# Masked prefix sums and a product: the blind pair in the third place of the ring, two rests a round, the last block summed by columns

## Chip, cores, metric

One core of a Trainium2 chip. The metric is the device time in microseconds of one execution, launch to end; four runs of the kernel before lie within 0.3% (84.62 to 84.87). The profile's span is from the first to the last instruction.

## The reference

```python
B, S, D = 8, 8192, 512          # x: [B, S, D] float32, lengths: [B] int64, w: [D, D]
mask = (pos < lengths[:, None, None])
cs = np.cumsum(x * mask, axis=1)
mid_features = cs[b_idx, lengths // 2, :]
return mid_features @ w          # [B, D]
```

Only one row of each running sum is used, so for each of the eight sequences the first `n = min(length // 2 + 1, length)` rows are summed, and the eight sums are multiplied with `w`. With the drawn lengths `n` is 570, 2690, 256, 2057, 905, 3772, 3859 and 571.

## The kernel before

Rows come in blocks of 512 (1 MB). TensorE sums a block by multiplying it with a matrix of zeros and ones (`cur`) into `s_ps`, four matmuls side by side. What is left of a sequence below 512 rows is a "rest", loaded into `rem` by ScalarE's queue. Two blocks are loaded blind, before the lengths are known, into a buffer of their own:

```python
first = sb("first", [P, BLIND, G, D])
xt = sb("xt", [P, NS, 2, G, D])          # ring of NS = 3 places, a pair of blocks in each
last = sb("last", [P, G, D])
rem = sb("rem", [P, NS, G, D])           # three rests a round
# ...
for b in range(BLIND):
    nc.sync.dma_start(out=first[:, b], in_=xf[b * S:b * S + BLK].rearrange("(p g) d -> p g d", g=G)).then_inc(s_first[b], 16)
```

SyncE loads a pair when its place is free (`s_free`). TensorE sums it, VectorE then writes the place's next weights and frees it:

```python
pe.addr_align(256, offset=80, max_nops=0)     # where TensorE's program starts
# ...
for b in range(BLIND):
    pe.wait_ge(s_first[b], 16)
    for j in range(G):
        add(j, cur_first[:, b], first[:, b, j])
with pe.Fori(0, rounds):
    for k in range(NS):
        pairs(pe, left, add_pair, k, k + 1)       # keep_busy, wait, 4 or 8 matmuls, done
        with pe.If_cmp(some, k + 1, "IS_GE"):     # a rest behind each pair
            take(pe, s_rem[k], 16 * (len(PARTS) + 1))
            # ... four matmuls
```

The last block of the last sequence is loaded at the very end in four pieces (rows 0 and 1 of each group of four, row 2, row 3 left, row 3 right). Its first piece goes into `s_ps` as all blocks do; a tick then releases VectorE, which copies `s_ps` to `s_sb`. The other pieces, and `s_sb` itself, are summed by columns into `t_ps`, which VectorE transposes for the product:

```python
with pe.If_cmp(has_last, 1, "IS_GE"):
    pe.wait_ge(s_last[0], 16)
    for j in range(4):
        add(j, e_last[:], last[:, j // 2], slice(D // 2 * (j % 2), D // 2 * (j % 2 + 1)))
tell()                                            # VectorE may copy s_ps
with pe.If_cmp(has_last, 1, "IS_GE"):
    pe.wait_ge(s_last[1], 16)
    for h in range(2):
        add_columns(h, e_last[:], last[:, 2])
    pe.wait_ge(s_last[2], 16)
    add_columns(0, e_last[:], last[:, 3])
pe.wait_ge(s_dve, DVE_ALL + 1)
add_columns(0, fold[:], s_sb[:]).then_inc(s_pe, 1)
# ... the second half the same way, then the product
```

Of the kernel before, what the change touches and what calls it, by code (L numbers as in the profile page):

```python
# [13 lines left out]
P = 128  # L14
# [3 lines left out]
def kernel(  # L18
# [47 lines left out]
    RR = -(-B // NS)  # L66
# [13 lines left out]
    def sem(name):  # L80
        return tc.alloc_semaphore(name)

    first = sb("first", [P, BLIND, G, D])
    xt = sb("xt", [P, NS, 2, G, D])
    last = sb("last", [P, G, D])
    rem = sb("rem", [P, NS, G, D])
    wt = sb("wt", [P, KC, D])
    lens1 = sb("lens1", [1, 2 * NS * RR], I32)
# [28 lines left out]
    cur_first = sb("cur_first", [P, BLIND, B])  # L117
# [9 lines left out]
    table = sb("table", [P, max(B * (WT + 1), NS * RR * WT)])  # L127
    cur_rem = sb("cur_rem", [P, NS, WT])
# [14 lines left out]
    s_rdone, s_rfree, s_rem = [[sem(f"{n}{q}") for q in range(NS)] for n in ("rdone", "rfree", "rem")]  # L143
    s_last = [sem(f"last{h}") for h in range(len(ENDS))]
    s_first = [sem(f"first{b}") for b in range(BLIND)]
# [14 lines left out]
    def rounds_of(eng, n, least):  # L160

        assert all((i + PER - 1) * 43 >> 8 == -(-i // PER) for i in range(ITEMS))
        to = eng.alloc_register(f"{eng.engine.name}_rounds")
        eng.reg_alu(to, n, PER - 1, ALU.add)
        eng.reg_alu(to, to, 43, ALU.mult)
        eng.reg_alu(to, to, 8, ALU.logical_shift_right)
        eng.reg_alu(to, to, least, ALU.max)
        return eng.snap(to, min_val=least, max_val=ROUNDS)
# [12 lines left out]
    nc.sync.dma_start(out=lens1[:, :2 * B], in_=lens_words).then_inc(s_len1, 16)  # L181
# [5 lines left out]
    for b in range(BLIND):  # L187
        nc.sync.dma_start(
            out=first[:, b], in_=xf[b * S:b * S + BLK].rearrange("(p g) d -> p g d", g=G)
        ).then_inc(s_first[b], 16)  # L190
# [70 lines left out]
    def _(act):  # L261
# [3 lines left out]
        words = [act.alloc_register(f"act_n{i}") for i in range(2 * NS)]  # L265
        pair, top = act.alloc_register("act_pair"), 2 * NS * (RR - 1)
        some = act.alloc_register("act_some")
        act.reg_mov(base, 0)
        act.reg_mov(pair, 0)
        act.reg_mov(some, B)  # L270
        act.memzero(lens1[:, 2 * B:])  # L271
        for q in range(NS):
            act.memzero(rem[:, q]).then_inc(s_rfree[q], 1)  # L273
        act.wait_ge(s_len1, 16)
        with act.Fori(0, RR):
            act.load(words, lens1[:, ds(act.snap(pair, min_val=0, max_val=top), 2 * NS)])
            def rest(q):

                n = words[2 * q]
                alu(t, n, 1, ALU.logical_shift_right)  # L280
                alu(t, t, 1, ALU.add)
                alu(n, t, n, ALU.min)
                take(act, s_rfree[q], 1)
                for count, start, step, g in PARTS:
                    alu(t, n, count, ALU.bitwise_and)
                    with act.If_cmp(t, 1, "IS_GE"):
                        alu(t, n, ~(2 * count - 1), ALU.bitwise_and)
                        act.dma_start(
                            out=rem[start::step, q, :g],
                            in_=rows(act, at, base, t, count).rearrange("(p g) d -> p g d", g=g),  # L290
                        ).then_inc(s_rem[q], 16)
                    with act.Else():
                        act.sem_inc(s_rem[q], 16)
                alu(at, n, ~63, ALU.bitwise_and)
                alu(at, at, base, ALU.add)
                alu(t, n, 63, ALU.bitwise_and)

                def load_last(count):
                    to = rem[3::4, q, 2:] if count > 32 else rem[3:4 * count:4, q, 2:3]
                    act.dma_start(  # L300
                        out=to,
                        in_=xf[ds(act.snap(at), count)].rearrange("(g p) d -> p g d", g=to.shape[1]),
                    ).then_inc(s_rem[q], 16)

                with act.If_cmp(t, 33, "IS_GE"):
                    load_last(64)
                with act.Else():
                    with act.If_cmp(t, 17, "IS_GE"):
                        load_last(32)
                    with act.Else():  # L310
                        with act.If_cmp(t, 1, "IS_GE"):
                            load_last(16)
                        with act.Else():
                            act.sem_inc(s_rem[q], 16)
                alu(base, base, S, ALU.add)
            for q in range(NS):
                if q < B - NS * (RR - 1):
                    rest(q)
                else:
                    with act.If_cmp(some, q + 1, "IS_GE"):  # L320
                        rest(q)
            less(act, some, NS)
            alu(pair, pair, 2 * NS, ALU.add)
            alu(pair, pair, top, ALU.min)
# [10 lines left out]
    def _(pool):  # L335
# [9 lines left out]
        for k in range(NS):  # L345
            pool.sem_inc(s_free[k], 1)
# [4 lines left out]
    def _(dve):  # L351
# [21 lines left out]
        step(dve.tensor_copy, out=len_f[:], in_=lens1[:, :2 * B:2])  # L373
# [8 lines left out]
        def addresses(a, b):  # L382
# [8 lines left out]
        step(dve.tensor_tensor, out=above[:], in0=shape(lens1[:, :2 * B:2].unsqueeze(2), 1, B, K), in1=steps[:],  # L391
# [15 lines left out]
        step(dve.memset, cur_first[:], 0.0)  # L407
# [13 lines left out]
        step(dve.tensor_copy, out=cur_first[:].rearrange("p k b -> p (k b)")[:, ::B + 1], in_=has[:, :BLIND])  # L421
# [6 lines left out]
        step(dve.tensor_tensor, out=cur[:].rearrange("p k h b -> p b (k h)"), in0=since[:, :B, BLIND:BLIND + PER],  # L428
             in1=since[:, 1:, BLIND:BLIND + PER], op=ALU.subtract)
# [14 lines left out]
        tab = table[:, :B * (WT + 1)].rearrange("p (b q) -> p b q", b=B)  # L444
# [4 lines left out]
        rests = table[:, :NS * RR * WT].rearrange("p (r q w) -> p r q w", q=NS, w=WT)  # L449
# [18 lines left out]
        dve.reg_mov(at, BLIND + PER)  # L468
        dve.reg_mov(of, 1)
        dve.reg_mov(some, B - NS)  # L470
        with dve.Fori(1, rounds_of(dve, left, RR)):
            less(dve, left, PER)

            def weights(k):
                take(dve, s_done[k], 1)
                here = ds(dve.snap(at, min_val=BLIND + PER, max_val=ITEMS - PER) + 2 * k, 2)
                dve.tensor_tensor(  # L477
                    out=cur[:, k], in0=since[:, :B, here].rearrange("p b h -> p h b"),
                    in1=since[:, 1:, here].rearrange("p b h -> p h b"), op=ALU.subtract,
                ).then_inc(s_free[k], 1)  # L480

            for k in range(NS):
                pairs(dve, left, weights, k, k + 1)
                with dve.If_cmp(some, k + 1, "IS_GE"):
                    take(dve, s_rdone[k], 1)
                    dve.tensor_copy(  # L486
                        out=cur_rem[:, k],
                        in_=rests[:, ds(dve.snap(of, min_val=1, max_val=RR - 1), 1), k].rearrange("p o w -> p (o w)"),
                    ).then_inc(s_rfree[k], 1)
            less(dve, some, NS)  # L490
            dve.reg_alu(at, at, PER, ALU.add)
            dve.reg_alu(at, at, ITEMS - PER, ALU.min)
            dve.reg_alu(of, of, 1, ALU.add)
            dve.reg_alu(of, of, RR - 1, ALU.min)
# [15 lines left out]
    def _(pe):  # L510
        def add(j, weights, rows, columns=slice(0, D)):

            return pe.matmul(s_ps[32 * j:32 * j + B, columns], lhsT=weights, rhs=rows[:, columns],  # L513
# [30 lines left out]
        left, some, has_last = [pe.alloc_register(f"pe_{n}") for n in ("left", "some", "has")]  # L544
        pe.wait_ge(s_dve, DVE_FIRST)
        pe.load([has_last, left], addr[:, :2])
        pe.reg_mov(some, B)
        rounds = rounds_of(pe, left, RR)
        for b in range(BLIND):
            pe.wait_ge(s_first[b], 16)  # L550
            for j in range(G):
                add(j, cur_first[:, b], first[:, b, j])
        BUSY = [3, 1, 0]
        pe.wait_ge(s_dve, DVE_MASK)
        with pe.Fori(0, rounds):
# [10 lines left out]
            for k in range(NS):  # L566
                pairs(pe, left, add_pair, k, k + 1)
                with pe.If_cmp(some, k + 1, "IS_GE"):
                    take(pe, s_rem[k], 16 * (len(PARTS) + 1))
                    for j in range(G):  # L570
                        mm = add(j, cur_rem[:, k, j * B:(j + 1) * B], rem[:, k, j])
                    mm.then_inc(s_rdone[k], 1)
            less(pe, left, PER)
            less(pe, some, NS)

        with pe.If_cmp(has_last, 1, "IS_GE"):
            pe.wait_ge(s_last[0], 16)
            for j in range(4):
                add(j, e_last[:], last[:, j // 2], slice(D // 2 * (j % 2), D // 2 * (j % 2 + 1)))
        tell()  # L580
        with pe.If_cmp(has_last, 1, "IS_GE"):
            pe.wait_ge(s_last[1], 16)
            for h in range(2):
                add_columns(h, e_last[:], last[:, 2])
# [52 lines left out]
```

## Time and profile before

| | before |
|---|---|
| time, median of the runs until then | 84.75 us |
| span | 82.4 us |
| moved by DMA | 31.25 MB, all engines full from 2.1 to 76.2 us |
| last ordinary block on TensorE | 74.82 us |
| first transpose | 77.37 us |

The prediction shows the slices and the tail. What it uses besides is when SyncE issues its loads (columns: start, duration, engine, line, operation). The first of these lines is the first load into the third place, the second the first refill of the ring:

```profile
10.48 0.34 SPq L222 DMA_DIRECT2D xt<-in_x_dram  x1
19.70 0.34 SPq L222 DMA_DIRECT2D xt<-in_x_dram  x1
```

### The profile page before, as it was taken

To read this page: it belongs to the slowest core of one execution; us is meant where nothing else is said; L and a number is where in the kernel's file an instruction comes from. 1 tells how busy PE (TensorE), PEld (TensorE's weight loads), DVE (VectorE), ACT (ScalarE), POOL (GpSimd) and SP (SyncE) were. 2 spreads that over 40 slices of the span, in tenths; PEclk is the share of its full clock that TensorE was granted. 3 is DMA by queue.
4 is the path that set the end of the run, shared out by engine and by line. 5 is a ranking of instruction groups with operands and counts; after the bars stand their busy time and mean duration, and the time that the engine had idled before them with its cause. 6 is when DMAs were issued, how large, how long until landed. Compare 5 with 4: busy or idle time off the path is not lost. (4 is left out here: it accounts for less than half of the span.)

```text
span 82.4 us, 1513 instructions
## 1 busy us (share of the span) xinstructions
PE 57.7 (70%) x389; PEld 15.1 (18%) x389; DVE 15.0 (18%) x79; ACT 7.4 (9%) x8; POOL 1.3 (2%) x14
## 2 busy tenths in 40 slices
PE   2800699589089699992198099999957989196920
PEld 2300005021021114120011021422201422011510
DVE  2758887001000100010000000000000000000620
ACT  0999300000000000000000000000000000000020
POOL 5000000000000000000000000000000000000000
PEclk9999999999965999999858957999999999999997
DMA  1999999999999999999999999999999999999000
GB/s 18 360 396 420 461 406 429 462 418 398 450 438 404 392 461 390 406 424 408 448 404 422 434 453 419 433 414 438 438 398 461 430 398 453 390 402 377 17 2 6
DMA packets 3826, 31.25 MB, mean 379 GB/s; under 512 B 562, under 2 KB 834, under 8 KB 1618
## 3 DMA queue, kind: packets, MB, share of 16 engines
q1 hardware_dynamic: 2754, 27.27, 78.8%
q10 hardware_dynamic: 1072, 3.97, 12.4%
HBM read 31.23 MB, written 0.02 MB: 379 GB/s over the span
## 5 line engine op out<-in xcount | busy, mean ns | idle before, releaser
L513 PE MATMUL s_ps<-xt,cur 128*8 128x512 f32 x184 | 26.5, 699 | 14.3 <-PEq L151 14.3
L528 PE MATMUL idle_ps<-idle 128*128 128x512 f32 x32 | 16.2, 628 | 0.0
L513 PEld LDWEIGHTS s_ps<-xt,cur 128*8 128x8 f32 x184 | 4.3, 94 | 33.5 <-issue 33.5
L477 DVE TENSOR_TENSOR cur<-since 128x16 f32 x9 | 1.7, 188 | 44.4 <-DVEq L151 44.4
L513 PE MATMUL s_ps<-rem,cur_rem 128*8 128x512 f32 x64 | 8.6, 610 | 0.0
L528 PEld LDWEIGHTS idle_ps<-idle 128*128 128x128 f32 x32 | 5.6, 196 | 11.7 <-issue 11.7
L513 PE MATMUL s_ps<-first,cur_first 128*8 128x512 f32 x16 | 3.6, 1040 | 5.0 <-DVE since L360 5.0
L329 ACT COPY o_sb<-o_ps 8x128 f32<-8x128 f32 x2 | 0.5, 260 | 69.9 <-PE o_ps L600 69.9
L273 ACT ACTIVATE rem<-rem 128x2048 uint32<-128x2048 uint32 x3 | 5.5, 1892 | 0.0
L513 PEld LDWEIGHTS s_ps<-rem,cur_rem 128*8 128x8 f32 x64 | 2.0, 102 | 7.0 <-issue 7.0
L539 PE MATMUL s_ps<-zero 1*128 1x512 f32 x2 | 2.1, 1137 | 1.6 <-DVE zero L360 1.6
L360 DVE COPY s_sb<-s_ps 128x256 f32<-128x256 f32 x2 | 0.8, 424 | 11.6 <-PE idle_ps L532 11.5
L486 DVE COPY cur_rem<-table 128x32 f32 x5 | 0.9, 182 | 3.2 <-DVEq L151 3.2
L513 PEld LDWEIGHTS s_ps<-first,cur_first 128*8 128x8 f32 x16 | 0.2, 89 | 6.7 <-issue 5.1
L271 ACT ACT_TABLE_LOAD x1 | 1.3, 1283 | 1.9 <-issue 1.9
L600 PE MATMUL o_ps<-wt,t_sb 128*8 128x128 f32 x32 | 1.1, 273 | 0.1
L360 DVE TENSOR_TENSOR part_a<-since,step_a 1x42 f32<-1x42 f32 (+1 forms) x2 | 1.1, 565 | 0.1
L521 PE MATMUL t_ps<-last,e_last 128*8 128x64 f32 x32 | 1.0, 220 | 0.1
L360 DVE TENSOR_TENSOR since<-item,begin 1x42 f32<-1x42 int32 (+1 forms) x2 | 0.8, 422 | 0.1
L600 PEld LDWEIGHTS o_ps<-wt,t_sb 128*8 128x8 f32 x32 | 0.8, 89 | 0.3 <-issue 0.3
L542 PEld LDWEIGHTS n_ps<-len_f,ones 1*128 1x128 f32 x2 | 0.7, 332 | 1.0 <-DVE above L360 0.5
L539 PEld LDWEIGHTS s_ps<-zero 1*128 1x128 f32 x2 | 0.5, 306 | 1.6 <-DVE zero L360 1.6
(70 smaller groups left out, 14.3 us busy)
## 6 DMA issues: line engine op xcount, KB each, us to landing
xt<-in_x_dram SPq DMA_DIRECT2D x10, 2048.0 KB, 12.4
xt<-in_x_dram SPq DMA_DIRECT2D x3, 1024.0 KB, 9.5
first<-in_x_dram SPq DMA_DIRECT2D x2, 1024.0 KB, 7.6
rem<-in_x_dram ACTq DMA_DIRECT2D x3, 512.0 KB, 8.6
wt<-in_w_dram ACTq DMA_DIRECT2D x2, 512.0 KB, 5.5
rem<-in_x_dram ACTq DMA_DIRECT2D x3, 256.0 KB, 7.6
last<-in_x_dram SPq DMA_DIRECT2D x1, 512.0 KB, 7.6
rem<-in_x_dram ACTq DMA_DIRECT2D x3, 128.0 KB, 8.0
```

What stands on the lines that cost most here:

```text
L271: act.memzero(lens1[:, 2 * B:])
L273: act.memzero(rem[:, q]).then_inc(s_rfree[q], 1)
L329: copy = act.copy(out=o_sb[1][:, j * P:(j + 1) * P], in_=o_ps[64 + 32 * j:64 + 32 * j + B, :P])
L360: do(*args, **kw).then_inc(s_dve, 1)
L477: dve.tensor_tensor(out=cur[:, k], in0=since[:, :B, here].rearrange("p b h -> p h b"), in1=since[:, 1:, here].rearrange("p b h -> p h b"), ...
L486: dve.tensor_copy(out=cur_rem[:, k], in_=rests[:, ds(dve.snap(of, min_val=1, max_val=RR - 1), 1), k].rearrange("p o w -> p (o w)"),).then_ ...
L513: return pe.matmul(s_ps[32 * j:32 * j + B, columns], lhsT=weights, rhs=rows[:, columns], start=False, stop=False, skip_group_check=True, t ...
L521: mm = pe.matmul(t_ps[h][32 * j:32 * j + B, :P // 2], lhsT=weights, rhs=row[:, at:at + P // 2], start=False, stop=False, skip_group_check= ...
L528: pe.matmul(idle_ps[:], lhsT=idle[:], rhs=idle[:, :1].to_broadcast((P, D)), start=True, stop=True)
L539: pe.matmul(s_ps[:], lhsT=zero[:], rhs=zero[:, :1].to_broadcast((1, D)), start=True, stop=False, skip_group_check=True)
L542: pe.matmul(n_ps[:, :B], lhsT=ones[:], rhs=len_f[:], start=True, stop=True).then_inc(s_pe, 1)
L600: mm = pe.matmul(o_ps[32 * j:32 * j + B, :P], lhsT=t_sb[:, kc, :B], rhs=wt[:, kc, j * P:(j + 1) * P], start=(kc == 0), stop=(kc == KC - 1) ...
```

## The change

Intent: save the separate buffer and the separate code of the blind blocks by treating them as a pair that already stands in the third place, with a loop round of its own; take two rests a round instead of three; and take the last block's first piece off the way of the tick, by summing all its rows by columns.

```diff
-    RR = -(-B // NS)
+    NR = 2
+    RR = -(-B // NR)
-    first = sb("first", [P, BLIND, G, D])
-    rem = sb("rem", [P, NS, G, D])
+    rem = sb("rem", [P, NR, G, D])
     for b in range(BLIND):
         nc.sync.dma_start(
-            out=first[:, b], in_=...
-        ).then_inc(s_first[b], 16)
+            out=xt[:, NS - 1, b], in_=...
+        ).then_inc(s_full[NS - 1], 16)
 # ... GpSimd frees places 0 and 1 only; VectorE, behind its set-up:
+        pairs(dve, left, weights, NS - 1)
 # ... TensorE:
-        with pe.Fori(0, rounds):
-            for k in range(NS):
-                pairs(pe, left, add_pair, k, k + 1)
-                with pe.If_cmp(some, k + 1, "IS_GE"):
+        with pe.Fori(0, rounds_of(pe, left, RR + 1)):
+            with pe.If_cmp(begun, 1, "IS_GE"):
+                pe.wait_ge(s_dve, DVE_MASK)
+                for k in range(NR):
+                    pairs(pe, left, add_pair, k, k + 1)
+                    with pe.If_cmp(some, k + 1, "IS_GE"):
 # ...
+            pairs(pe, left, add_pair, NS - 1)
+            pe.reg_mov(begun, 1)
-        with pe.If_cmp(has_last, 1, "IS_GE"):
-            pe.wait_ge(s_last[0], 16)
-            for j in range(4):
-                add(j, e_last[:], last[:, j // 2], slice(...))
         tell()
         with pe.If_cmp(has_last, 1, "IS_GE"):
-            pe.wait_ge(s_last[1], 16)
-            for h in range(2):
-                add_columns(h, e_last[:], last[:, 2])
+            for i, some in enumerate(([0, 1], [2])):
+                pe.wait_ge(s_last[i], 16)
+                for g in some:
+                    for h in range(2):
+                        add_columns(h, e_last[:], last[:, g])
```

More of the change, by code (lines that the diff above doesn't have):

```diff
@@ L81, in sem @@
         return tc.alloc_semaphore(name)
-    first = sb("first", [P, BLIND, G, D])
     xt = sb("xt", [P, NS, 2, G, D])
     last = sb("last", [P, G, D])
-    rem = sb("rem", [P, NS, G, D])
+    rem = sb("rem", [P, NR, G, D])
     wt = sb("wt", [P, KC, D])
-    lens1 = sb("lens1", [1, 2 * NS * RR], I32)
+    lens1 = sb("lens1", [1, 2 * B], I32)
     len_f = sb("len_f", [1, B])
@@ L116 @@
     row_last = sb("row_last", [1, 1], I32)
-    cur_first = sb("cur_first", [P, BLIND, B])
     cur = sb("cur", [P, NS, 2, B])
@@ L126 @@
     thr = sb("thr", [P, G], I32)
-    table = sb("table", [P, max(B * (WT + 1), NS * RR * WT)])
-    cur_rem = sb("cur_rem", [P, NS, WT])
+    table = sb("table", [P, B * (WT + 1)])
+    cur_rem = sb("cur_rem", [P, NR, WT])
     fold_i = sb("fold_i", [P, B], I32)
@@ L142 @@
     s_done, s_free, s_full = [[sem(f"{n}{k}") for k in range(NS)] for n in ("done", "free", "full")]
-    s_rdone, s_rfree, s_rem = [[sem(f"{n}{q}") for q in range(NS)] for n in ("rdone", "rfree", "rem")]
+    s_rdone, s_rfree, s_rem = [[sem(f"{n}{q}") for q in range(NR)] for n in ("rdone", "rfree", "rem")]
     s_last = [sem(f"last{h}") for h in range(len(ENDS))]
-    s_first = [sem(f"first{b}") for b in range(BLIND)]
     s_w, s_len1, s_out = sem("w"), sem("len1"), sem("out")
@@ L167, in rounds_of @@
         eng.reg_alu(to, to, least, ALU.max)
-        return eng.snap(to, min_val=least, max_val=ROUNDS)
+        return eng.snap(to, min_val=least, max_val=ROUNDS + 1)
     def less(eng, n, by):
@@ L178 @@
     PE_ALL, PE_SUM, PE_OUT = 2, 3, 5
-    nc.sync.dma_start(out=lens1[:, :2 * B], in_=lens_words).then_inc(s_len1, 16)
+    nc.sync.dma_start(out=lens1[:], in_=lens_words).then_inc(s_len1, 16)
     for h in range(2):
@@ L188 @@
         nc.sync.dma_start(
-            out=first[:, b], in_=xf[b * S:b * S + BLK].rearrange("(p g) d -> p g d", g=G)
-        ).then_inc(s_first[b], 16)
+            out=xt[:, NS - 1, b], in_=xf[b * S:b * S + BLK].rearrange("(p g) d -> p g d", g=G)
+        ).then_inc(s_full[NS - 1], 16)
     block = nc.Block(no_gpsimd_drain=True)
@@ L264, in _ @@
         base, at, t = [act.alloc_register(f"act_{n}") for n in ("base", "at", "t")]
-        words = [act.alloc_register(f"act_n{i}") for i in range(2 * NS)]
-        pair, top = act.alloc_register("act_pair"), 2 * NS * (RR - 1)
-        some = act.alloc_register("act_some")
+        words = [act.alloc_register(f"act_n{i}") for i in range(2 * NR)]
+        pair, top = act.alloc_register("act_pair"), 2 * NR * (RR - 1)
         act.reg_mov(base, 0)
         act.reg_mov(pair, 0)
-        act.reg_mov(some, B)
-        act.memzero(lens1[:, 2 * B:])
-        for q in range(NS):
+        for q in range(NR):
             act.memzero(rem[:, q]).then_inc(s_rfree[q], 1)
@@ L275, in _ @@
         with act.Fori(0, RR):
-            act.load(words, lens1[:, ds(act.snap(pair, min_val=0, max_val=top), 2 * NS)])
+            act.load(words, lens1[:, ds(act.snap(pair, min_val=0, max_val=top), 2 * NR)])
             def rest(q):
@@ L315, in rest @@
                 alu(base, base, S, ALU.add)
-            for q in range(NS):
-                if q < B - NS * (RR - 1):
-                    rest(q)
-                else:
-                    with act.If_cmp(some, q + 1, "IS_GE"):
-                        rest(q)
-            less(act, some, NS)
-            alu(pair, pair, 2 * NS, ALU.add)
+            for q in range(NR):
+                rest(q)
+            alu(pair, pair, 2 * NR, ALU.add)
             alu(pair, pair, top, ALU.min)
@@ L344, in _ @@
         pool.iota(fold_i[:], pattern=[[-1, B]], base=128, channel_multiplier=1).then_inc(s_pool, 1)
-        for k in range(NS):
+        for k in range(NS - 1):
             pool.sem_inc(s_free[k], 1)
@@ L372, in _ @@
         dve.wait_ge(s_len1, 16)
-        step(dve.tensor_copy, out=len_f[:], in_=lens1[:, :2 * B:2])
+        step(dve.tensor_copy, out=len_f[:], in_=lens1[:, ::2])
         assert done == DVE_N, done
@@ L390, in _ @@
         dve.wait_ge(s_pool, 1)
-        step(dve.tensor_tensor, out=above[:], in0=shape(lens1[:, :2 * B:2].unsqueeze(2), 1, B, K), in1=steps[:],
+        step(dve.tensor_tensor, out=above[:], in0=shape(lens1[:, ::2].unsqueeze(2), 1, B, K), in1=steps[:],
              op=ALU.is_ge)
@@ L406, in _ @@
         step(dve.memset, since[:, B:], 0.0)
-        step(dve.memset, cur_first[:], 0.0)
+        step(dve.memset, cur[:], 0.0)
         step(dve.memset, bits[:], 256)
@@ L419, in _ @@
              op0=ALU.is_ge, op1=ALU.mult)
-        step(dve.tensor_copy, out=cur_first[:].rearrange("p k b -> p (k b)")[:, ::B + 1], in_=has[:, :BLIND])
+        step(dve.tensor_copy, out=cur[:, NS - 1].rearrange("p h b -> p (h b)")[:, ::B + 1], in_=has[:, :BLIND])
         step(dve.tensor_copy, out=addr[:, :1], in_=has[:1, B - 1:])
@@ L427, in _ @@
         sinces(begin, 0, ITEMS)
-        step(dve.tensor_tensor, out=cur[:].rearrange("p k h b -> p b (k h)"), in0=since[:, :B, BLIND:BLIND + PER],
-             in1=since[:, 1:, BLIND:BLIND + PER], op=ALU.subtract)
+        step(dve.tensor_tensor, out=cur[:, :NS - 1].rearrange("p k h b -> p b (k h)"),
+             in0=since[:, :B, BLIND:PER], in1=since[:, 1:, BLIND:PER], op=ALU.subtract)
         step(dve.tensor_scalar, out=m4[:], in0=pid[:], scalar1=3, scalar2=None, op0=ALU.bitwise_and)
@@ L443, in _ @@
         step(dve.tensor_tensor, out=thr[:, 2:], in0=thr_i[:], in1=shape(m4[:], P, 2), op=ALU.mult)
-        tab = table[:, :B * (WT + 1)].rearrange("p (b q) -> p b q", b=B)
+        tab = table[:].rearrange("p (b q) -> p b q", b=B)
         step(dve.tensor_tensor, out=cap[:], in0=shape(cnt[:].unsqueeze(2), P, B, G),
@@ L448, in _ @@
              in1=shape(thr[:].unsqueeze(1), P, B, G), op=ALU.is_gt)
-        rests = table[:, :NS * RR * WT].rearrange("p (r q w) -> p r q w", q=NS, w=WT)
+        rests = table[:, :B * WT].rearrange("p (r q w) -> p r q w", q=NR, w=WT)
         step(dve.tensor_copy, out=cur_rem[:], in_=rests[:, 0])
@@ L467, in _ @@
         dve.load([left], addr[:, 1:2])
-        dve.reg_mov(at, BLIND + PER)
+        dve.reg_mov(at, BLIND)
         dve.reg_mov(of, 1)
-        dve.reg_mov(some, B - NS)
-        with dve.Fori(1, rounds_of(dve, left, RR)):
-            less(dve, left, PER)
-            def weights(k):
-                take(dve, s_done[k], 1)
-                here = ds(dve.snap(at, min_val=BLIND + PER, max_val=ITEMS - PER) + 2 * k, 2)
-                dve.tensor_tensor(
-                    out=cur[:, k], in0=since[:, :B, here].rearrange("p b h -> p h b"),
-                    in1=since[:, 1:, here].rearrange("p b h -> p h b"), op=ALU.subtract,
-                ).then_inc(s_free[k], 1)
+        dve.reg_mov(some, B - NR)
@@ new lines, in _, with weights @@
+        rounds = rounds_of(dve, left, RR)
+        def weights(k):
+            take(dve, s_done[k], 1)
+            here = ds(dve.snap(at, min_val=BLIND, max_val=ITEMS - PER) + 2 * k, 2)
+            dve.tensor_tensor(
+                out=cur[:, k], in0=since[:, :B, here].rearrange("p b h -> p h b"),
+                in1=since[:, 1:, here].rearrange("p b h -> p h b"), op=ALU.subtract,
+            ).then_inc(s_free[k], 1)
+        pairs(dve, left, weights, NS - 1)
+        with dve.Fori(1, rounds):
+            less(dve, left, PER)
+            dve.reg_alu(at, at, PER, ALU.add)
+            dve.reg_alu(at, at, ITEMS - PER, ALU.min)
@@ L482, in _ @@
             for k in range(NS):
                 pairs(dve, left, weights, k, k + 1)
-                with dve.If_cmp(some, k + 1, "IS_GE"):
-                    take(dve, s_rdone[k], 1)
-                    dve.tensor_copy(
-                        out=cur_rem[:, k],
-                        in_=rests[:, ds(dve.snap(of, min_val=1, max_val=RR - 1), 1), k].rearrange("p o w -> p (o w)"),
-                    ).then_inc(s_rfree[k], 1)
-            less(dve, some, NS)
-            dve.reg_alu(at, at, PER, ALU.add)
@@ L492, in _ @@
-            dve.reg_alu(at, at, ITEMS - PER, ALU.min)
+                if k < NR:
+                    with dve.If_cmp(some, k + 1, "IS_GE"):
+                        take(dve, s_rdone[k], 1)
+                        dve.tensor_copy(
+                            out=cur_rem[:, k],
+                            in_=rests[:, ds(dve.snap(of, min_val=1, max_val=RR - 1), 1), k].rearrange("p o w -> p (o w)"),
+                        ).then_inc(s_rfree[k], 1)
+            less(dve, some, NR)
             dve.reg_alu(of, of, 1, ALU.add)
@@ L510, in _, with add @@
     def _(pe):
-        def add(j, weights, rows, columns=slice(0, D)):
-            return pe.matmul(s_ps[32 * j:32 * j + B, columns], lhsT=weights, rhs=rows[:, columns],
+        def add(j, weights, rows):
+            return pe.matmul(s_ps[32 * j:32 * j + B], lhsT=weights, rhs=rows,
                              start=False, stop=False, skip_group_check=True,
@@ L543, in _ @@
         pe.wait_ge(s_pool, 2)
-        left, some, has_last = [pe.alloc_register(f"pe_{n}") for n in ("left", "some", "has")]
+        left, some, has_last, begun = [pe.alloc_register(f"pe_{n}") for n in ("left", "some", "has", "begun")]
+        pe.reg_mov(some, B)
+        pe.reg_mov(begun, 0)
         pe.wait_ge(s_dve, DVE_FIRST)
         pe.load([has_last, left], addr[:, :2])
-        pe.reg_mov(some, B)
-        rounds = rounds_of(pe, left, RR)
-        for b in range(BLIND):
-            pe.wait_ge(s_first[b], 16)
-            for j in range(G):
-                add(j, cur_first[:, b], first[:, b, j])
+        pe.reg_alu(left, left, PER, ALU.add)
         BUSY = [3, 1, 0]
-        pe.wait_ge(s_dve, DVE_MASK)
-        with pe.Fori(0, rounds):
+        with pe.Fori(0, rounds_of(pe, left, RR + 1)):
             def add_pair(k):
@@ L564, in add_pair @@
                 mm.then_inc(s_done[k], 1)
-            for k in range(NS):
-                pairs(pe, left, add_pair, k, k + 1)
-                with pe.If_cmp(some, k + 1, "IS_GE"):
-                    take(pe, s_rem[k], 16 * (len(PARTS) + 1))
-                    for j in range(G):
-                        mm = add(j, cur_rem[:, k, j * B:(j + 1) * B], rem[:, k, j])
-                    mm.then_inc(s_rdone[k], 1)
-            less(pe, left, PER)
-            less(pe, some, NS)
-        with pe.If_cmp(has_last, 1, "IS_GE"):
-            pe.wait_ge(s_last[0], 16)
-            for j in range(4):
-                add(j, e_last[:], last[:, j // 2], slice(D // 2 * (j % 2), D // 2 * (j % 2 + 1)))
+            with pe.If_cmp(begun, 1, "IS_GE"):
[3 more added lines that the diff above has]
+                    with pe.If_cmp(some, k + 1, "IS_GE"):
+                        take(pe, s_rem[k], 16 * (len(PARTS) + 1))
+                        for j in range(G):
+                            mm = add(j, cur_rem[:, k, j * B:(j + 1) * B], rem[:, k, j])
+                        mm.then_inc(s_rdone[k], 1)
+                less(pe, some, NR)
+            pairs(pe, left, add_pair, NS - 1)
+            less(pe, left, PER)
+            pe.reg_mov(begun, 1)
         tell()
         with pe.If_cmp(has_last, 1, "IS_GE"):
-            pe.wait_ge(s_last[1], 16)
-            for h in range(2):
-                add_columns(h, e_last[:], last[:, 2])
+            for i, some in enumerate(([0, 1], [2])):
[3 more added lines that the diff above has]
+                        add_columns(h, e_last[:], last[:, g])
             pe.wait_ge(s_last[2], 16)
```

## The prediction

> **What bounds the kernel now.** I read the page first, its slices by time and its DMA queues.
>
> ```profile
> PE   2800699589089699992198099999957989196920
> DMA  1999999999999999999999999999999999999000
> GB/s 18 360 396 420 461 406 429 462 418 398 450 438 404 392 461 390 406 424 408 448 404 422 434 453 419 433 414 438 438 398 461 430 398 453 390 402 377 17 2 6
> q1 hardware_dynamic: 2754, 27.27, 78.8%
> q10 hardware_dynamic: 1072, 3.97, 12.4%
> ```
>
> One slice is 82.4/40 = 2.06 us. The sixteen DMA engines are full from the second slice to the 37th (2.1 to 76.2 us), and the two queues add up to 91.2% of 16 engines' span, 75 us: all of that time. TensorE shows a nine often too, but with gaps throughout, and 16.2 us of its work are matmuls on `idle`[...]. So the kernel is a 31.25 MB transfer at about 420 GB/s, with a head of some 2 us before the stream starts and a tail of some 6 us after it. A change can gain only by (a) fewer bytes, (b) fewer holes in the stream, (c) a shorter tail.
>
> The DMA queue's own waits, that is those of the engine that issues the loads, say why the stream has no holes:
>
> ```profile
> SPq L151 <- SPq L151: 32.0, 9, 6.6
> SPq L239 <- DVE fold L360: 3.6, 1, 3.6
> ```
>
> It stands 32 us waiting for a place in the ring of three pairs, with work for the engines already queued. So a place freed a microsecond later costs nothing until the queue behind it runs empty.
>
> The tail I read from the timeline of its last microseconds (start, duration, engine, what, and in brackets the idle time before it):
>
> ```profile
> 74.82 1.04 PE L513 MATMUL s_ps<-xt,cur 128*8 128x512 f32 x8 [0.74 <-PEq L151]
> 75.69 0.62 PE L513 MATMUL s_ps<-last,e_last 128*8 128x256 f32 x8
> 76.13 0.17 PE L532 MATMUL idle_ps<-tick 128*1 128x1 bf16 x1
> 76.36 0.49 PEld L521 LDWEIGHTS t_ps<-last,e_last 128*8 128x8 f32 x24 [0.37 <-DMA last<-in_x_dram]
> 76.39 0.88 DVE L360 COPY s_sb<-s_ps 128x256 f32<-128x256 f32 x2 [11.53 <-PE idle_ps L532]
> 77.32 0.30 PE L521 MATMUL t_ps<-s_sb,fold 128*8 128x64 f32 x8
> 77.37 0.61 DVE L360 STREAM_TRANSPOSE t_sb<-t_ps 128x64 f32<-128x64 f32 x2
> 77.77 1.06 PE L600 MATMUL o_ps<-wt,t_sb 128*8 128x128 f32 x32
> ```
>
> The last ordinary block reaches TensorE at 74.82, the first half of the last block is added by 76.13, then comes the tick that lets VectorE copy `s_ps`. The two copies end at 77.27; only then can VectorE start the transposes (77.37), and the product follows. In that half microsecond the copies bind, not the transfer: by the windows the DMA share is 1.03 in 75 to 76 us, 0.32 in 76 to 77 and 0 after it.
>
> [...]
>
> **The change part by part.**
>
> *Bytes.* By the diff the same loads are issued: 2 blind blocks, 12 pairs (10 as one load of 2048 KB, one as two, and a single block), 8 rests, the last block in four. Nothing is saved or added: 0 us.
>
> *The third place starts occupied.* Before, the load into it was issued at 10.48 us. Now it waits until both blind blocks have been summed and VectorE has written new weights.
> - TensorE: the blind blocks landed 6.3 and 8.9 us after their issues at 1.3 and 1.7, so the second is there at 10.6. Before, the first one's 8 matmul passes ran from 8.87, while the second still came; now all 16 start at 10.6 and take about 3.6 us[...]. They end near 14.2 instead of 12.5.
> - VectorE: it must first finish its set-up, whose last step ended at 14.62, then load registers and branch. TensorE needed 1.3 us for the like (from 7.53 to its first matmul at 8.86). Then the 0.19 us subtraction: free at about 16.2.
> - Issue: before, from a place freed at 19.12 to the load at 19.70 is 0.58 us. So the load goes out near 17 us, 6.5 us later than before, with data about 1.5 us on (the first issues at 0.9 met a full stream only after 2.06): 18.3 us.
> - What lies queued until then, in decimal MB: weights 1.05, blind 2.10, two pairs 4.19, the two rests 0.43, together 7.77. The stream of before had moved 5.8 MB by 16 us and 7.46 by 20 (windows of 2 us: 16, 344, 389, 426, 479, 427, 433, 393, 446, 377 GB/s), so the queue would run dry at about 20.7 us. That is 2.4 us after the new data start. On paper the cost is **0**. I chose to charge **0.1 us**, as the engines don't run level: the second pair was summed only from 23.03 although the bytes ahead of it had passed some 2 us before, so a few engines may stand still briefly.
> - TensorE then does its three keep-busy rounds (3.15 us) from 14.2, so the first pair starts at about 17.3, not 16.72. The load that follows it goes out near 20.2, not 19.70, with a whole pair still queued: **0**.
>
> *Two rests a round.* Eight rests take four rounds instead of three. The pairs take four rounds anyway (23 blocks in rounds of six), and the last rests are summed in the last of them. A rest lands 6 to 8 us after its issue and has a round of about 15 us for it. ScalarE has two memzeros instead of three (1.89 us each) and issues its first rest earlier: before the queues drain, so **0**.
>
> *The blind round.* TensorE runs its loop five times; the extra branches fall where it waits for the blind data: **0**.
>
> *The tail.* Four 256-column matmuls (8 passes, 75.69 to 76.13, 0.44 us) become sixteen 64-column ones behind the tick. The 24 passes in the fence load in 0.49 us, 20.4 ns each, so 32 passes are 0.65 us.
> - The tick moves from 76.13 to 75.69, the copies from 76.39 to about 75.95, and end at 76.83 instead of 77.27.
> - TensorE: 32 passes to 76.35; the third row group (landed about 76.33), 16 passes, to 76.68; the first half of the fourth, 8 passes, to 76.84; fold of the first half to 77.00; last columns to 77.17; second fold to 77.33.
> - The first transpose needs the first fold's end, 76.84 + 0.30 = 77.14, plus the same 0.1 us: 77.24 instead of 77.37. The product and the rest follow, each earlier by **0.13 us**.
>
> So the gain is not the 0.44 us that VectorE wins, as TensorE's longer column work becomes the wait. Sum: -0.13 + 0.1, about 0; from 84.75 I say **84.7 us**.
>
> **The rivals.**
> - *The stream gets a hole* because two pairs instead of three lie queued at the start. For it: the place is freed 6.5 us later, and VectorE's long set-up stands before it. Against it: 2.4 us of reserve. If data come at 21.5 us rather than 18.3, it costs up to 0.8 us: 85.5. A hole would cost its whole length, since the stream is the bound.
> - *TensorE becomes the bound of the tail*: if small column passes run slower than 20.4 ns, at say 30, the 56 passes ahead of the first fold cost 0.5 us more: 85.2. Against it: these very passes are in the trace before.
> - *The stream gets better or worse by itself*, as the rests mix in another order with the pairs: slices vary from 390 to 462 GB/s. One per cent of 74 us is 0.7 us, either way; 84.0 to 85.4.
> - *A full tail gain of 0.44 us*, if the last pieces land earlier so that TensorE is never behind: 84.3.
>
> **Range and chances.** The runs before span 0.25 us. With the mix worth ±0.7 and a hole possibly 0.8, I take 84.0 to 85.4. Two per cent is 1.7 us: no rival alone brings it. Faster by more than 2% would need fewer bytes or a higher rate: 2%. Slower by more than 2% needs a hole of 1.7 us: 4%. Within 2%: 94%.
>
> **What would show it.** In the changed trace: the load into the third place issued at about 17 us; the GB/s of the slices between 14 and 24 us still near 420 (a slice under 300 shows the hole); the DMA bytes still 31.25 MB, the stream ending near 76.3; the tick directly behind the last block's matmuls, 0.4 us earlier relative to them; the first transpose about 2.4 us after the last ordinary block's first matmul (before 2.55). I am wrong if the stream ends over 0.5 us from 76.3, or if column passes take more than 0.65 us for the first half.

-0.13 us for the tail and +0.1 us charged for a brief stand of some engines come to about 0, and from 84.75 to 84.7 us. The 3.6 us for the blind pair are the 3.64 us that its 16 passes took in the profile before (1040 ns each, where the rests' take 610). That the DMA engines don't run level was an estimate from the sums at 23.03 us; the trace doesn't record which engine moved what.

## The result

The changed kernel took 84.07 us (84.00 to 84.18, 4 runs), the kernel before 84.73 us (84.62 to 84.87, 4 runs). The ratio is 0.992 (95% interval 0.990 to 0.994). A ratio here is the mean time of one kernel's fast runs over that of the other's in the same rounds, so it is not quite the ratio of the medians. Executions over 1.5% slower than the fastest of the same kernel are left out of the means. Measured once more with more runs (below) it was 0.995 (0.992 to 0.998): a gain of 0.4 to 0.7 us, inside the predicted range, at its lower end.

The page of the changed kernel, slices and queues:

```profile
GB/s 20 355 414 420 440 438 427 441 414 398 462 414 434 426 422 370 426 450 426 430 406 418 454 382 452 434 408 422 442 420 420 402 450 454 370 410 379 27 0 8
q1 hardware_dynamic: 2754, 27.27, 79.0%
q10 hardware_dynamic: 1072, 3.97, 12.3%
```

The bytes are the same, and no slice between 14 and 24 us (the seventh to the twelfth) falls under 398: the stream has no hole. The head, from the timelines (TensorE's blind pair and its keep-busy matmuls, VectorE's weights that free the third place, the load into it):

```profile
11.00 3.60 PE L506 MATMUL s_ps<-xt,cur 128*8 128x512 f32 x16 [7.12 <-DVE thr L350]
14.53 2.85 PE L521 MATMUL idle_ps<-idle 128*128 128x512 f32 x6
16.20 0.18 DVE L466 TENSOR_TENSOR cur<-since 128x16 f32 x1 [1.62 <-DVEq L149]
16.95 0.34 SPq L220 DMA_DIRECT2D xt<-in_x_dram  x1
```

The load goes out at 16.95 us, where the prediction said "near 17". The tail:

```profile
74.93 1.05 PE L506 MATMUL s_ps<-xt,cur 128*8 128x512 f32 x8
75.79 0.17 PE L525 MATMUL idle_ps<-tick 128*1 128x1 bf16 x1
75.81 0.45 PEld L514 LDWEIGHTS t_ps<-last,e_last 128*8 128x8 f32 x32 [0.30 <-DMA last<-in_x_dram]
76.08 0.88 DVE L350 COPY s_sb<-s_ps 128x256 f32<-128x256 f32 x2 [10.46 <-PE idle_ps L525]
76.50 0.45 PEld L514 LDWEIGHTS t_ps<-last,e_last 128*8 128x8 f32 x24 [0.23 <-DMA last<-in_x_dram]
77.31 0.60 DVE L350 STREAM_TRANSPOSE t_sb<-t_ps 128x64 f32<-128x64 f32 x2 [0.35 <-PE t_ps L514]
```

The stream delivers the last ordinary block 0.11 us later than in the profile before (74.93, 74.82), the tick follows it at once, and the first transpose starts 2.38 us after that block's first matmul instead of 2.55: 0.17 us gained. So the two profiles differ by 0.1 us of span. The gain of the runs is larger than that of the profiled pair: this is what the experiments had to look into.

### The profile page after: what moved, and what is told of

Read it like the earlier page. It is cut to its first block, busy times and chain, and to the rows that moved or that the text cites. A ratio compares the mean times of both kernels' runs of the same rounds, so it can differ in the third digit from the quotient of the medians.

```text
span 82.3 us, 1574 instructions
## 1 busy us (share of the span) xinstructions
PE 55.7 (68%) x413; PEld 15.6 (19%) x413; DVE 15.3 (19%) x81; ACT 5.5 (7%) x6; POOL 1.3 (2%) x14
## 2 busy tenths in 40 slices
DMA packets 3826, 31.25 MB, mean 380 GB/s; under 512 B 562, under 2 KB 834, under 8 KB 1618
## 3 DMA queue, kind: packets, MB, share of 16 engines
q1 hardware_dynamic: 2754, 27.27, 79.0%
## 5 line engine op out<-in xcount | busy, mean ns | idle before, releaser
L506 PE MATMUL s_ps<-xt,cur 128*8 128x512 f32 x200 | 28.0, 681 | 21.3 <-PEq L149 14.2
L521 PE MATMUL idle_ps<-idle 128*128 128x512 f32 x32 | 16.8, 648 | 0.0
L268 ACT ACTIVATE rem<-rem 128x2048 uint32<-128x2048 uint32 x2 | 3.7, 1901 | 0.0
L514 PE MATMUL t_ps<-last,e_last 128*8 128x64 f32 x64 | 1.6, 220 | 0.0
L514 PEld LDWEIGHTS t_ps<-last,e_last 128*8 128x8 f32 x64 | 0.9, 88 | 0.7 <-DMA last<-in_x_dram 0.5
L350 DVE TENSOR_REDUCE sum_a<-part_a 1x6 f32<-1x42 f32 (+1 forms) x2 | 0.8, 381 | 0.1
```

Source lines behind the costliest of these rows:

```text
L268: act.memzero(rem[:, q]).then_inc(s_rfree[q], 1)
L350: do(*args, **kw).then_inc(s_dve, 1)
L506: return pe.matmul(s_ps[32 * j:32 * j + B], lhsT=weights, rhs=rows, start=False, stop=False, skip_group_check=True, tile_position=(0, 32 * j))
L514: mm = pe.matmul(t_ps[h][32 * j:32 * j + B, :P // 2], lhsT=weights, rhs=row[:, at:at + P // 2], start=False, stop=False, skip_group_check= ...
L521: pe.matmul(idle_ps[:], lhsT=idle[:], rhs=idle[:, :1].to_broadcast((P, D)), start=True, stop=True)
```

## The experiments

Two theories at the start. **A**: the whole gain is the tail. **B**: the tail gives what its trace shows, and the rest comes from the stream, through the occupied third place or through the later rests. The first four runs take the parts one by one; all ran on one chip with five rounds.

### The tail alone

The kernel before, with only the last hunk of the diff above.

> The kernel before with the new tail alone (all rows of the last block by columns behind the tick; blind blocks in their own buffer, three rests a round). Theory A, the whole gain of 0.66 us (84.73 to 84.07) is the tail: 84.1 us, ratio 0.992. Theory B, the tail gives only the 0.13 us worked out in the prediction and the rest comes from an earlier end of the stream: 84.6 us, ratio 0.998. The first transpose should come some 2.4 us after the first matmul of the last ordinary block (before 2.55).

Measured: 85.31 us, ratio 1.008 (1.005 to 1.012): 0.8% longer, clear of the noise. Neither theory had this. The tail itself works as it should; the last ordinary block came late:

```profile
76.41 1.04 PE L513 MATMUL s_ps<-xt,cur 128*8 128x512 f32 x8 [0.73 <-PEq L151]
78.77 0.61 DVE L360 STREAM_TRANSPOSE t_sb<-t_ps 128x64 f32<-128x64 f32 x2 [0.34 <-PE t_ps L521]
```

From one to the other are 2.36 us, as in the changed kernel; but the block is there 1.6 us later than before (76.41, 74.82). All six runs have spans of 83.3 to 83.8 us. The page names one queue that the pages of before and of the changed kernel lack. From the DMA view of 32 to 34 us (packets, MB, share of sixteen engines):

```profile
q8 instruction: 1, 0.02, 3.3%
```

One instruction transfer, beside the stream. 3.3% of 16 engines' 2 us are 1.06 us of one engine. And the windows at the end (length; busy times of PE, PEld, DVE, ACT and POOL; granted clock; DMA share; GB/s) show a share of about one engine still at work, here against the changed kernel, which is the second fence:

```profile
76.75:77.50 0.75, 0.75 (x25) 0.31 (x21) 0.00 (x0) 0.00 (x0) 0.00 (x0) 1.00 0.07 26
```

```profile
76.75:77.50 0.75, 0.75 (x44) 0.46 (x32) 0.40 (x2) 0.00 (x0) 0.00 (x0) 1.00 0.00 0
```

A share of 0.06 to 0.07 is about one engine of sixteen. Which one, the trace doesn't record; that it is the engine of the transfer is inferred. The kernel waits for all sixteen counts of a load (`wait_ge(s_last[0], 16)`), and the trace has sixteen landings for that load, in the changed kernel from 75.19 to 75.77 us. So the last of the sixteen decides when a load is there.

### The old tail in the changed kernel

The changed kernel with the old hunk of the tail put back.

> The changed kernel with the old tail (first half of the last block into s_ps ahead of the tick). Theory A: no gain left, 84.7 us, ratio 1.000. Theory B: most of the gain stays, 84.2 us, ratio 0.994, with the first transpose about 2.55 us after the last ordinary block's first matmul.

Measured: 84.54 us, ratio 1.000 (0.996 to 1.004). The profile has the old tail's length, 77.49 less 74.93 = 2.56 us:

```profile
74.93 1.04 PE L506 MATMUL s_ps<-xt,cur 128*8 128x512 f32 x8
77.49 0.60 DVE L350 STREAM_TRANSPOSE t_sb<-t_ps 128x64 f32<-128x64 f32 x2
```

So theory B falls in the form that I gave it: the other two parts together bring no gain that this resolves. The new tail gains with them and didn't without them; why, the next runs try to find out.

### Two rests a round alone

The kernel before with `NR = 2`, everything else as before.

> The kernel before with two rests a round alone (blind blocks keep their own buffer, old tail). Theory A: 84.7 us, ratio 1.000. Theory B with the rests' later loads as its cause (they mix with the pairs over the whole stream): 84.3 us, ratio 0.994. Theory B with the occupied third place as its cause: 84.7, ratio 1.000.

Measured: 84.55 us, ratio 0.998 (0.994 to 1.003). No effect resolved.

### The blind pair in the third place alone

The changed kernel with `NR = 3`, the third rest behind the third pair, and the old tail.

> The kernel before with the blind pair in the third place alone (three rests a round as before, the third rest behind the third pair, old tail). Theory A: 84.7 us, ratio 1.000. Theory B with the occupied third place as its cause: 84.3 us, ratio 0.994; with the rests as its cause: 84.7 us, ratio 1.000. The third place's first load goes out near 17 us in either case.

Measured: 84.44 us, ratio 0.998 (0.995 to 1.001); the load into the third place went out at 16.99 us. No effect resolved, as the prediction had it.

### What the other parts do for the tail

The new tail needs 12 matmuls more in TensorE's program. The two other parts save exactly as many: 4 for the third rest and 8 for the blind blocks. I counted the matmuls in the built programs: 95 before, 95 in the changed kernel, 107 with the tail alone. Each fp32 matmul is four instructions (the ring's 23 blocks, four matmuls each, are 184 weight loads and 184 passes on the page of before), and behind the alignment directive the three programs have 444, 443 and 489 instructions. With a start at slot 80 they end at slots 524, 523 and 569; the last instructions of before and of the changed kernel run after the product. The next expectations rest on an assumption of mine that no run had shown: that a program which ends early enough brings no instruction transfer into the stream.

Hence **theory F**: placement and length of TensorE's program decide whether an instruction transfer falls into the stream, and such a transfer costs about a microsecond (by the spans of the tail alone, 83.53 less 82.48). Its rival **G**: the longer column work disturbs the stream in some other way. The next runs move programs without altering an instruction.

### The changed kernel again

> The changed kernel once more, unaltered. Its runs so far had spans of 82.1 to 82.4 us where the kernel before had 82.2 to 82.6 in most of its runs, so the spans differ by some 0.15 us, while the times outside the span scatter by 0.6 us. If the -0.66 us of the first four runs was part scatter: 84.3 to 84.4 us, ratio 0.995 to 0.998. If it is real: 84.0, ratio 0.992.

Measured: 84.14 us (84.03 to 84.28, 6 runs), before 84.56 (11 runs), ratio 0.995 (0.992 to 0.998). The spans are 82.2 to 82.5 us (mean 82.32), those of before 82.4 to 82.6 and once 83.5 (mean 82.56). So of 0.44 us, the difference of the means, 0.24 lie in the span (0.17 of them the tail of the profile, 0.07 more within what single runs scatter), and 0.20 outside it, where before took 1.8 to 2.3 us and the changed kernel 1.75 to 2.0. An instruction transfer shows in this profile too, but only in the window behind 79 us, when the stream has ended; the profile of before has one there as well, at 83.6 us, behind its last instruction. There the stream is not longer: the span of this profile is 82.3 us, that of before 82.4. From the DMA view of before, 83.5 to 84.6 us:

```profile
q8 instruction: 1, 0.02, 5.3%
```

That is 0.93 us of one engine, with no stream beside it.

### The tail alone, placed 48 slots earlier

```diff
-        pe.addr_align(256, offset=80, max_nops=0)
+        pe.addr_align(256, offset=32, max_nops=0)
```

> The tail-only kernel that was 0.8% slower, its TensorE program merely placed 48 instruction slots earlier (offset 32 instead of 80). Theory F: that kernel lost 1.2 us[...]. Then here the instruction transfer is gone from the DMA part of the page, the span is 82.2 to 82.3 us (82.4 less the 0.13 us of the tail), ratio 0.995 to 0.998. Rival G: the longer column work itself, with three rests and separate blind buffers, slows the stream: again 83.5 us of span, ratio 1.008.

Measured: 85.27 us, ratio 1.008 (1.004 to 1.012), spans 83.0 to 83.7. A miss: the transfer did not go away. It came earlier (DMA view of 2 to 3 us):

```profile
q8 instruction: 1, 0.02, 5.7%
```

So an earlier end of the program (slot 521, below the 524 of before) doesn't keep a transfer out of the stream; that part of theory F falls. That the stream is late when a transfer falls into it stands (span 83.33, before 82.56).

### The changed kernel, placed 48 slots later

> The changed kernel with its TensorE program placed 48 slots later (offset 128 instead of 80)[...]. Theory F: one instruction transfer shows in the DMA part of the page, the span is 83.3 to 83.7 us, 1.2 us longer than the changed kernel's, ratio to the kernel before about 1.009. Rival G: no change, span 82.2, ratio 0.995.

Measured: 85.58 us, ratio 1.013 (1.008 to 1.017), spans 83.4 to 83.8. The instructions are those of the changed kernel, so a loss of this size needs no longer column work, and theory G isn't needed. For the tail alone G isn't excluded: no run of it was free of a transfer. In the DMA view of 12 to 14 us, and in the window at the end:

```profile
q8 instruction: 1, 0.02, 3.1%
```

```profile
76.75:77.50 0.75, 0.75 (x12) 0.22 (x8) 0.00 (x0) 0.00 (x0) 0.00 (x0) 1.00 0.06 23
```

### The third place freed late

This tests the step of the prediction that mattered most, the reserve of the queue. Nine memsets on VectorE, each waiting for the one before, stand between its set-up and the blind pair's weights.

```diff
         dve.wait_ge(s_dve, done)
+        for i in range(9):
+            if i:
+                dve.wait_ge(s_late, i)
+            dve.memset(s_sb[:], 0.0).then_inc(s_late, 1)
+        dve.wait_ge(s_late, 9)
```

> The changed kernel with nine extra memsets on VectorE between its set-up and the blind pair's weights (some 5 to 6 us), so that the third place is freed near 22 us instead of 16.4 and its load goes out near 22.5. By the prediction the queues are empty at about 20.7 us and new data come 1.4 us after the issue, near 24: a hole of some 3 us in the stream, seen as slices well under 400 GB/s between 18 and 24 us, and 87 us (ratio 1.03). If a freed place has no such deadline (rival: the engines are never short of work, as the other places refill them), the time stays at 84.3 and the slices near 420.

Measured: 88.32 us, ratio 1.044 (1.040 to 1.047), spans 86.2 to 86.5. The load's issue, and the windows around it:

```profile
22.93 0.34 SPq L221 DMA_DIRECT2D xt<-in_x_dram  x1
```

```profile
18.00:20.00 2.00, 2.00 (x21) 0.56 (x24) 1.46 (x3) 0.00 (x0) 0.00 (x0) 1.00 1.04 442
20.00:22.00 2.00, 2.00 (x14) 0.41 (x10) 0.48 (x1) 0.00 (x0) 0.00 (x0) 1.00 0.16 66
22.00:24.00 2.00, 2.00 (x24) 0.44 (x16) 0.55 (x3) 0.00 (x0) 0.00 (x0) 1.00 0.18 41
24.00:26.00 2.00, 0.52 (x8) 0.00 (x0) 0.37 (x2) 0.00 (x0) 0.00 (x0) 1.00 0.86 229
```

The stream runs dry soon after 20 us and is thin or empty until about 24; the span grows by 4.0 us (mean 86.34 less 82.32). The deadline is real, a hole costs about its length, and it lies about where the prediction had it (20.7). The load went out 6.0 us later than in the changed kernel (22.93, 16.95) and the span grew by 4.0. So by estimate the changed kernel's load had some 2.0 us to spare, not 2.4.

### The kernel before, placed 16 slots earlier

> The kernel before with its TensorE program placed 16 slots earlier (offset 64)[...]. The open question: before, the time outside the span scatters from 1.8 to 2.3 us, in the changed kernel from 1.75 to 2.0. If those last instructions cause it, here the span stays 82.4 us and the time drops to 84.2 (ratio 0.996). If not: 84.55, ratio 1.000.

"Those last instructions" are the last 12 of the program, slots 512 to 523 in the kernel before.

Measured: 86.14 us, ratio 1.019 (1.014 to 1.023), spans 84.1 to 85.0. Again the same instructions as the kernel before, and again a transfer in the stream (DMA view of 2 to 4 us) with the share of about one engine still at work at the end:

```profile
q8 instruction: 1, 0.02, 5.4%
```

```profile
77.50:78.50 1.00, 1.00 (x13) 0.34 (x14) 0.00 (x0) 0.00 (x0) 0.00 (x0) 1.00 0.06 24
```

So for the kernel before, too, the place of the program alone costs time. But with offset 64 its 444 instructions end at slot 508, earlier than before, and here a transfer falls into the stream that before lacks: a second miss for my assumption. The run does not answer the question for which it was made: the time outside the span was 1.88 us on average, and on that chip that of before was 1.89 too.

### One engine held by data

The kernel before with one more load, of 17 rows of 1 KB, meant to lie on one DMA engine.

```diff
         act.wait_ge(s_len1, 16)
+        act.dma_start(out=extra[:], in_=xf[:17, :D // 2]).then_inc(s_extra, 16)
```

> The kernel before with one added transfer of 17 rows of 1 KB[...], issued at about 7 us; its data are not used. Theory F: holding one of sixteen engines for some 0.7 to 1.3 us makes that engine lag to the end of the stream[...]: the DMA share stays near 0.06 (one engine of sixteen) for about a microsecond behind 76.5 us, span 83.1 to 83.7, ratio 1.006 to 1.012. Rival: 17 KB of 31 MB is 0.06%, 0.04 us; span 82.4, ratio 1.000.

Measured: 84.66 us, ratio 1.002 (0.996 to 1.008); five fast runs with spans of 82.7 to 83.5 (mean 82.92, before 82.69). The cost is 0.2 us, less than expected and hardly resolved. By the rate of the stream, 27.27 MB in 78.8% of 16 engines' 82.4 us or 26 GB/s an engine, 17.4 KB are an estimated 0.7 us. The trace has 17 packets of 1 KB between 8.5 and 16.6 us, never two at once, as on one engine, of 46 to 52 ns each, 0.8 us together. The shortest instruction transfer in the stream took 0.9 us and went with 0.8 us of span. So the one direct test of the mechanism, an engine held makes the stream late, is mostly a miss: neither bytes nor held time alone explain the loss. What else an instruction transfer does, or whether the engine of this test had time to spare, stays open.

### The tail alone, placed 64 slots earlier

> The tail-only kernel with its TensorE program at offset 16[...]. Theory F: no instruction transfer during the stream, span 82.2 to 82.3 us as the changed kernel, ratio 0.995 to 0.998; the first transpose 2.36 us after the last ordinary block's first matmul. So the tail alone would give the changed kernel's gain, and the two other parts only make room for it. Rival G: span 83.0 to 83.8 as in the two other tail-only runs.

Measured: 86.07 us, ratio 1.016 (1.011 to 1.021), spans 83.7 to 84.7, a transfer between 2 and 4 us. A third miss for my assumption: with offset 16 the program ends at slot 505, well ahead of the 524 of before, and still an instruction transfer falls into the stream. At 16, 32 and 64 the transfer comes at 2 to 4 us; at 80 it stays out of the stream for the programs of 444 and 443 instructions, and at 80 with 489 and at 128 with 443 it comes later. So a clean run of the tail alone, without a transfer, I could not make.

### The first fold ahead of half a row

The changed kernel, with one column half of the third row group (8 passes) moved behind the first fold.

> The changed kernel with the second column half of the last block's third row group summed behind the first fold instead of ahead of it: 8 passes of 20 ns leave the way to the first transpose. If TensorE binds there, the first transpose comes 0.16 us earlier (2.22 us after the last ordinary block's first matmul instead of 2.38); if the landing of the fourth row group's first half binds, 0.0 to 0.08 us earlier. Ratio to the kernel before 0.993 to 0.995 either way, so the trace decides, not the time.

Measured: 84.55 us, ratio 1.001 (0.995 to 1.007), spans 82.2 to 83.3 (before on that chip 82.3 to 83.3). The trace, by which it was to be judged:

```profile
74.90 1.04 PE L506 MATMUL s_ps<-xt,cur 128*8 128x512 f32 x8
76.82 0.12 PEld L514 LDWEIGHTS t_ps<-last,e_last 128*8 128x8 f32 x8 [0.24 <-DMA last<-in_x_dram]
77.30 0.60 DVE L350 STREAM_TRANSPOSE t_sb<-t_ps 128x64 f32<-128x64 f32 x2 [0.37 <-PE t_ps L514]
```

From block to transpose are 2.40 us, against 2.38: nothing gained. The passes taken off the way are replaced by a wait for the fourth row group, which lands at about 76.8. The first fold is at the landing's limit. No version of mine beat the changed kernel, so none is proposed.

### The runs together

| run | instruction transfer in the stream, engine held | span, mean of fast runs | before, same rounds | ratio |
|---|---|---|---|---|
| tail alone, slot 80 | 32 to 34 us, 1.06 us | 83.53 | 82.48 | 1.008 |
| old tail | none | 82.37 | 82.48 | 1.000 |
| two rests alone | none | 82.53 | 82.48 | 0.998 |
| blind pair alone | none | 82.57 | 82.48 | 0.998 |
| changed kernel again | none | 82.32 | 82.56 | 0.995 |
| tail alone, slot 32 | 2 to 3 us, 0.91 us | 83.33 | 82.56 | 1.008 |
| changed kernel, slot 128 | 12 to 14 us, 0.99 us | 83.57 | 82.56 | 1.013 |
| third place late | none | 86.34 | 82.56 | 1.044 |
| before, slot 64 | 2 to 4 us, 1.73 us | 84.40 | 82.69 | 1.019 |
| 17 KB meant for one engine | none | 82.92 | 82.69 | 1.002 |
| tail alone, slot 16 | 2 to 4 us, 1.41 us | 84.20 | 82.69 | 1.016 |
| first fold early | none | 82.70 | 82.69 | 1.001 |

The second column is from the one profile of each run's series. The held time is the share of sixteen engines by the length of the view, as worked out for the first. All five with a transfer in the stream are 0.8 to 1.7 us of span longer than before, and of the others only the one with the hole is that. The two with the longest held times are also the two slowest of the five, so among these five the lag follows the time that the engine is held, roughly, though the 17 KB of data, 0.8 us in all, cost only 0.2; in the profiled runs themselves the loss is 0.8 to 1.7 times the held time (for example 85.0 less 82.4 for 1.73, 83.0 less 82.3 for 0.91).

## Why the prediction was right, and where it was not

- **The bound.** Right: the same 31.25 MB, the stream full to 76.2 us; the hole made on purpose lengthened the span by 4.0 us. The 34 full slices from 4.1 to 74.2 us of the profile before run from 390 to 462 GB/s, with a mean of 423, near the prediction's "about 420".
- **The third place.** Right in its working: the blind pair ended at 14.6 (predicted 14.2), the weights were written by 16.38 (16.2), the load went out at 16.95 (17), the first refill at 20.31 (20.2). The 0.1 us charged for a brief stand of some engines was not seen; the blind pair alone came out at 0.998. The reserve was some 2.0 us rather than 2.4.
- **Two rests a round.** Right: 0.998, nothing resolved.
- **The tail.** Right in result, 0.17 us for 0.13, wrong in one step. The prediction took 20.4 ns for each small pass and concluded that "TensorE's longer column work becomes the wait". The 20.4 ns are a misreading: the 24 weight loads in 0.49 us stand in two groups with a wait between them. Windows of the profile before, with the weight loads of `last` alone (in brackets how many touch the window):

```profile
76.50:76.60 0.10, 0.09 (x8) 1.00 0.01 0
76.60:76.70 0.10, 0.00 (x0) 1.00 0.00 0
76.70:76.80 0.10, 0.06 (x8) 1.00 0.00 0
```

  The second group waits for the fourth row group's first half, which landed at 76.70. In the changed kernel the first 32 passes went by in 0.45 us, 14 ns each, not 0.65, and TensorE waited for data 0.30 us before them and 0.23 behind them. The landing binds the first fold, as the last experiment shows.
- **The parts as a sum.** Wrong as a way of thinking, though it didn't spoil the number. I added the parts as if each stood alone. The tail alone makes the kernel 0.8% slower; with the other two parts it gains. No rival of mine was a matter of program length, though the directive for the program's place stood in the code and should have made me ask what moving it does.
- **The size.** Predicted 84.7, measured 84.07 and again 84.14. Against the repeated pair (-0.44 us) the sum of -0.03 lacks 0.41: 0.1 for the charge that was not due, 0.04 of the tail, 0.07 of span within the scatter, and 0.20 outside the span, which the profile doesn't show. The cause of the last was not found, and it may belong to the chip: on the chip of the last four runs the kernel before took 1.89 us there instead of 2.03 to 2.12, so that less could be gained. Nor does it go with one part: against 2.12 us for before on their chip, the blind pair alone had 1.83 outside the span, the old tail in the changed kernel 2.20.

What is shown: the tail shortens by 0.17 us; the place of the program alone makes two kernels 1.25 and 1.7 us longer in span, and an instruction transfer then lies in the stream, as it does in all three runs of the tail alone. What is argued only: that the transfer causes the loss by holding its engine, and that the other two parts give the tail room; the matmul counts fit (12 for 12), but a tail-only program free of transfers was not reached. Open: what decides when an instruction transfer is made, and how a transfer costs the stream so much more than data of like size. Its own length is no effect of the stream: alone, behind it, one took 0.93 us.

## What to carry to other kernels

When one stream of transfers sets the time, as here, a buffer that comes free later can cost nothing up to the point where the queue runs dry (a load 6.5 us later: ratio 0.998), and costs about the length of the hole beyond it (6.0 us later still: 4.0 us of span): work out that point from the bytes queued and the rate, and then delay it on purpose to test it. Before adding instructions to a loop program that runs beside a saturated stream, look for an instruction queue on the page and for the time of its transfer (the five kernels here that had one in the stream were 0.8 to 1.7 us longer in span; no count of instructions foretold it): a change that looks neutral may be what makes room for another, and single-part trials that shift a program can mislead.
